# Final norm over all tiles with two experts still to come; the rows of the last two experts gathered, finished and written row by row into the output

## The chip, the cores and the metric

The kernel runs on one core of a Trainium2 chip. The time is device microseconds (us) of one execution. Five engines matter: TensorE (PE in the rows; its weight loads are PEld), VectorE (DVE), ScalarE (ACT), GpSimd (POOL) and SyncE (SP, which issues the plain DMAs). GpSimd also issues the indirect DMAs, which gather or scatter rows by a list of indices.

## What is computed

One layer of a decoder: a token mixer, then a mixture of 32 experts in which each token goes to two experts of one group, and a final RMS norm over the result. Only the end matters here:

```
out = jnp.zeros_like(tok)
for e in range(N_EXPERTS):
    hid = jax.nn.silu(tok @ w_gate[e]) * (tok @ w_up[e])
    out = out + combine[:, e:e + 1] * (hid @ w_down[e])
...
x = x + gate_f * out
return rmsnorm(x, norm_final)
```

with `rmsnorm(x, g) = x * rsqrt(mean(x * x) + EPS) * g`, over rows of 1024 values in f32. There are 1024 tokens, so the final norm has eight tiles of 128 rows.

## The kernel before

The kernel writes its instructions through a small scheduler of its own (`Sched`): each piece of work is a generator, which yields when it has to wait (for a time, or for a mark in `done`), and a modelled clock decides in which order the pieces put their instructions on the engines. On the chip each engine then runs its instructions in that order and waits on semaphores.

After the mixer and the router the residual rows stand in `x2d` in device memory and the normed rows in `h2d`. Each expert has a list of up to 96 tokens (`CAP`; `lists` holds tokens and weights, `LI["tok"]` the indices). For expert e the kernel gathers the listed rows of `h2d` (`gather`, an indirect DMA from GpSimd), transposes them on TensorE, multiplies by gate and up in three f32r passes, forms the product, multiplies by down (`down_gen`), and scales the result by the token's weight and gate row on VectorE (`y_gen`, `stt` into tile `y`). For experts 0 to 29 the 96 rows of `y` are then added to `x2d` by an indirect DMA that accumulates (`scatter`); each scatter waits until the one before has landed. The weights of all experts, 3 MB each, are loaded by SP and split in two on ScalarE and VectorE.

The last two experts, 30 and 31 (`NL = 2`), are not scattered. When the scatter of expert 29 is under way, `out_gen` starts: SP loads the eight tiles of `x2d` (into the weight buffers shown as HG, `fx` in the code) and the gain of the final norm (`nf`, shown as dn). The rows of experts 30 and 31 are put in place by TensorE instead: `sel_gen` has built, for each of the two, a 0/1 matrix that takes list places to tokens, and `y_mm` multiplies it with the two halves of `y` (tile `yw`, shown as ewx), eight matmuls for each of the eight output tiles. `out_fin` then handles a tile: add the loaded rows, square with a sum on ScalarE, the reciprocal root on GpSimd (`rstd_of`: a TENSOR_SCALAR and a TENSOR_TENSOR with pow, on 128x1), multiply by root and gain (one SCALAR_TENSOR_TENSOR on VectorE, for tiles 1 and 3 one on ScalarE and two on GpSimd), and store by SP into the output. No tile can be finished before expert 31 is multiplied by its down weights.

Of the kernel before, what the change touches and what calls it, by code (L numbers as in the profile page):

```python
# [19 lines left out]
P = 128  # L20
# [256 lines left out]
def build(tc, A, CB, CM, coff, out):  # L277
# [1452 lines left out]
    def gather(dst, idx):  # L1730
        LI["gat"] = G.indirect_dma_start(out=dst, out_offset=None, in_=h2d,
                             in_offset=bass.IndirectOffsetOnAxis(ap=idx, axis=0),
                             bounds_check=S - 1, oob_is_err=False)
        sch.note(G, 1.04)
        return sch.dma(dst.shape[0] * D * 4)
# [69 lines left out]
    def y_gen(e, py):  # L1805
# [13 lines left out]
        if e < NE - NL:  # L1819
# [9 lines left out]
            return  # L1829
        yw = yield from ews.take()  # L1830
# [7 lines left out]
        yts.put(y)  # L1838
        LI[("y", e)] = yw
        done.add(("y", e))  # L1840

    def sel_gen(mw):
        yield lambda: ("xT0", NE - NL + 1) in done
        for i in range(NL):
            sel = mw.tile([P, D], F32R, name="sel%d" % i, tag="xg%d" % i, bufs=1)
            tf, d8 = small([CAP, 1], "tf"), small([CAP, NT], "d8")
            ts(G, tf, lists[:, 0, EO[NE - NL + i]:EO[NE - NL + i] + 1], float(TOK0), OP.add)
            yield None
            ts(G, d8, iot[0:CAP, 0:NT], -float(P), OP.mult)
            ts(G, d8, d8, tf, OP.add)  # L1850
            yield None
            tt(V, sel[0:CAP].rearrange("p (t c) -> p t c", t=NT),
               iot[0:CAP, None, :].to_broadcast([CAP, NT, P]),
               d8[:, :, None].to_broadcast([CAP, NT, P]), OP.is_equal)
            LI["sel", i] = sel
            yield SEL_GAP
        done.add("sel")

    def out_gen():
# [12 lines left out]
        def slot(t):  # L1872
            if "pyL" in done and lvs.free():
                return lvs, 1
            if mms.free() > 1:
                return mms, 2
            if "hTL" in done and mss.free() > 1:
                return mss, 2

        for t in range(NT):  # L1880
            if t >= AHEAD:
                yield lambda: ("ym", t - AHEAD) in done
            yield lambda: slot(t) is not None
            res, n = slot(t)
            held = [res.tile() for _ in range(n)]
            p = held if n == 2 else [held[0][:, 0], held[0][:, 1]]
            if t in PREP:
                yield (f_at[t],)
                if "pyL" not in done:
                    yield lambda: "pyL" in done  # L1890
                for n in range(2):
                    mm(p[n], ident, fx[t][:, n * 512:(n + 1) * 512], True, False)
                yield (T_.free - LEAD,)
            for i in range(NL - 1):
                yield lambda: ("y", NE - NL + i) in done and "sel" in done
                y_mm(p, i, t, t not in PREP and i == 0)
                yield (T_.free - LEAD,)
            add(out_fin(t, res, held, p, fx[t], max(f_at[t], nf_at), nf))
            yield 0.0

    def y_mm(p, i, t, start):
        yw = LI[("y", NE - NL + i)]
        for h in range(2):
            for n in range(2):
                mm(p[n], LI["sel", i][0:CAP, t * P:(t + 1) * P], yw[0:CAP, h, n * 512:(n + 1) * 512],
                   start and h == 0, i == NL - 1 and h == 1)

    def out_fin(t, res, held, p, x, at, nf):
        yield lambda: ("y", NE - 1) in done and (t == 0 or ("ym", t - 1) in done)
        y_mm(p, NL - 1, t, False)  # L1910
        done.add(("ym", t), sch.t)
        yield (T_.free + LAT,)
        yield (at,)
        sq, rs = small([P, 2], "fsq"), small([P, 1], "frs")
        jk = nf[:, 1]
        if len(held) == 1:
            cols, p = [slice(0, D)], [held[0].rearrange("p b c -> p (b c)")]
        else:
            cols = [slice(0, 512), slice(512, D)]
        if t not in PREP:  # L1920
            for c, q in zip(cols, p):
                tt(V, x[:, c], q, x[:, c], OP.add)
            res.put(*held)
            yield None
            act(jk, x, AF.Square, accum_out=sq[:, 0:1])
            cols, p = [slice(0, D)], [x]
        else:
            for n, (c, q) in enumerate(zip(cols, p)):
                act(jk[:, c], q, AF.Square, accum_out=sq[:, n:n + 1])
            if len(p) > 1:  # L1930
                yield None
                tt(G, sq[:, 0:1], sq[:, 0:1], sq[:, 1:2], OP.add)
# [3 lines left out]
        if t >= NT - 1 and len(cols) == 1:  # L1936
            cols = [slice(0, 512), slice(512, D)]
            p = [p[0][:, c] for c in cols]
        for c, q in zip(cols, p):
            if t in POOL_T:  # L1940
                act(x[:, c], q, AF.Copy, scale=rs)
            else:
                stt(x[:, c], q, rs, nf[:, 0, c], OP.mult, OP.mult)
# [3 lines left out]
        if t in PREP:  # L1947
            res.put(*held)
# [335 lines left out]
```

## Time and profile before

| what | value |
|---|---|
| timed runs | 1141.23, 1144.24, 1150.05 us; median 1144.24 us |
| profiled execution | 1140.17 us, of which the span (first to last instruction) 1138.4 us |
| TensorE busy in the span | 1024.2 us (90%) |
| VectorE busy | 833.2 us (73%) |
| ScalarE busy | 521.3 us (46%) |
| GpSimd busy | 301.1 us (26%) |
| moved by DMA | 218.98 MB, mean 192 GB/s |
| mean granted TensorE clock | 0.966 |

Read it so: the profiler writes down one execution, with the start and the length of each instruction, and puts down each idle stretch of an engine to what ended it. Averages over the span say little about the last 40 us, where the change is made, so that stretch is read by itself. For an indirect DMA the length of the GpSimd instruction is not the transfer's; "to landing" is from its start until the data is there.

### The profile page before, as it was taken

Reading aid. Unit: us, or ns where it says so; the run is one execution under the profiler, and the core shown is the slowest. Engines: PE = TensorE matmul, PEld = TensorE weight load, DVE = VectorE, ACT = ScalarE, POOL = GpSimd, SP = SyncE. Lnnn points to the kernel's source line nnn. Section 1 sums busy time; section 2 is a strip of 40 time slices with the busy share of each in tenths; the row PEclk is TensorE's granted clock in tenths of the full one; section 3 lists DMA queues with packets and bytes.
Section 4 is the critical chain, followed back from the end, with each engine's and each line's share of the span. In section 5 each row is a group of like instructions: output and inputs, shape, how many; then the busy total and the mean of one; then the engine's idle time right before and its main releaser. Section 6 shows DMA issues by size and latency. Waiting matters only on the chain. (4 is left out here: it accounts for less than half of the span.)

```text
span 1138.4 us, 17044 instructions
## 1 busy us (share of the span) xinstructions
PE 1024.2 (90%) x6168; PEld 836.1 (73%) x6168; DVE 833.2 (73%) x1488; ACT 521.3 (46%) x981; POOL 301.1 (26%) x331
## 2 busy tenths in 40 slices
PE   3889999999989899998999998669999999999995
PEld 3779998899879888897898898546556555555554
DVE  6995776899997845459889887667666665757667
ACT  5423324556734323246555554355544444545434
POOL 4411220134411211102342212422332233433225
PEclk9899999999999999999999999879999999999998
DMA  9665557223214522134511189658999999999976
GB/s 310 188 190 186 163 165 237 56 56 94 80 42 132 169 83 56 43 100 131 172 56 57 55 295 337 237 153 254 298 293 322 305 318 308 316 319 317 312 227 260
DMA packets 96038, 218.98 MB, mean 192 GB/s; under 512 B 13342, under 2 KB 56538, under 8 KB 95954
## 3 DMA queue, kind: packets, MB, share of 16 engines
q1 hardware_dynamic: 89010, 201.67, 53.6%
q0 software_dynamic: 6944, 16.22, 6.3%
q8 instruction: 49, 0.80, 0.3%
q14 instruction: 35, 0.29, 0.1%
HBM read 201.64 MB, written 24.38 MB: 199 GB/s over the span
## 5 line engine op out<-in xcount | busy, mean ns | idle before, releaser
L220 PE MATMUL mm<-wg,HT 128*128 128x384 f32 (+2 forms) x1920 | 351.3, 335 | 19.3 <-DVE tmp L220 6.6
L220 PEld LDWEIGHTS mm<-wg,HT 128*128 128x128 f32 x1920 | 312.8, 193 | 31.1 <-issue 12.4
L220 PE MATMUL mm<-ew,xT 128*96 128x512 f32 x576 | 166.4, 427 | 7.8 <-DVE ew L220 6.1
L220 ACT ACTIVATE wg<-raw 128x768 fp32r<-128x768 f32 (+2 forms) x115 | 89.8, 782 | 144.3 <-PE mm L220 89.8
L220 DVE TENSOR_TENSOR wg<-raw,wg 128x768 fp32r<-128x768 f32 (+2 forms) x115 | 102.4, 890 | 62.2 <-ACT wg L220 61.8
L220 PEld LDWEIGHTS mm<-ew,xT 128*96 128x96 f32 x576 | 91.9, 165 | 61.6 <-issue 16.8
L220 DVE TENSOR_TENSOR ew<-HG,ew 128x1024 fp32r<-128x1024 f32 x68 | 81.3, 1218 | 34.3 <-ACT ew L220 34.3
L220 PE MATMUL lv<-rx 64*128 64x64 f32 (+5 forms) x1216 | 100.7, 278 | 5.5 <-DVE rx L220 3.7
L220 PEld LDWEIGHTS lv<-rx 64*128 64x128 f32 (+2 forms) x1216 | 89.1, 183 | 21.7 <-issue 15.0
L220 POOL DMA_INDIRECT x2d<-y,tki x30 | 64.7, 2158 | 144.6 <-DVE y L220 67.4
L220 PE MATMUL mm<-HT,wg 128*128 128x256 f32 (+1 forms) x576 | 97.2, 324 | 0.1
L220 ACT ACTIVATE ew<-HG 128x1024 fp32r<-128x1024 f32 x67 | 68.7, 1051 | 55.3 <-DMA HG<-expert_w_up 46.0
L220 PEld LDWEIGHTS mm<-HT,wg 128*128 128x128 f32 x576 | 82.1, 190 | 9.1 <-issue 1.0
L220 ACT ACTIVATE rx<-rx 128x64 f32<-128x64 f32 (+4 forms) x180 | 68.6, 418 | 31.8 <-DVE rx L220 19.6
L220 POOL DMA_INDIRECT xg<-h2d,tki x32 | 42.6, 1332 | 109.1 <-PE ms L220 98.2
L220 DVE SCALAR_TENSOR_TENSOR y<-lv,lists,GF 96x512 f32<-96x512 f32 x64 | 44.9, 740 | 31.2 <-PE lv L220 31.2
L220 PE MATMUL lv<-dn,hT 128*96 128x512 f32 x128 | 61.8, 606 | 2.0 <-ACT hT L220 2.0
L220 PE MATMUL lv<-dg,hT 128*96 128x512 f32 x128 | 60.1, 594 | 2.8 <-ACT hT L220 2.8
L220 PE MATMUL mm<-ewx,xT 128*96 128x512 f32 x192 | 59.9, 447 | 2.2 <-DVE ewx L220 2.0
L220 DVE TENSOR_TENSOR rx<-rx,qkc 128x320 f32<-128x320 f32 (+4 forms) x109 | 57.7, 563 | 0.8 <-ACT rx L220 0.8
L220 POOL TENSOR_TENSOR rx<-rx,qkc 128x256 f32<-128x256 f32 (+2 forms) x19 | 20.9, 1100 | 134.0 <-ACT rx L220 132.0
L220 PEld LDWEIGHTS ms<-cst,xg 96*128 96x128 f32 x256 | 34.5, 204 | 23.1 <-issue 13.3
(301 smaller groups left out, 1611.4 us busy)
## 6 DMA issues: line engine op xcount, KB each, us to landing
raw<-w_in SPq DMA_DIRECT2D x64, 384.0 KB, 3.3
HG<-expert_w_gate SPq DMA_DIRECT2D x46, 512.0 KB, 7.2
HG<-expert_w_up SPq DMA_DIRECT2D x46, 512.0 KB, 7.8
h<-w_ada SPq DMA_DIRECT2D x32, 512.0 KB, 4.4
dn<-expert_w_down SPq DMA_DIRECT2D x32, 512.0 KB, 8.4
dg<-expert_w_down SPq DMA_DIRECT2D x32, 512.0 KB, 8.8
raw<-w_out SPq DMA_DIRECT2D x26, 384.0 KB, 3.4
gu<-expert_w_gate SPq DMA_DIRECT2D x18, 512.0 KB, 6.4
```

The lines of the kernel that those rows point to most:

```text
L220: r = f(*a, **k)
```

## The change

- `sel_gen`, `y_mm` and their matrices are gone: six small GpSimd instructions, two 96x1024 ones on VectorE, and the 64 matmuls of 512 columns of `y_mm` with the two that brought tile 0 into the accumulator.
- `out_fin` no longer waits for experts 30 and 31. It norms each tile of `x2d` as it stands after expert 29 and stores it: eight full stores.
- `late_gen` and `late_rows` are new. When the scatter of expert 29 has landed, the rows of `x2d` that experts 31 and 30 will change are gathered into `xf` (two indirect DMAs). For expert 30 its `y` is added to its rows, normed, and written row by row into the output by an indirect DMA (`rows_out`). A token may stand in both lists; so a 96x96 matrix `both` (one small matmul and two small VectorE instructions; two 128x1024 fills on VectorE clear the tiles of the gathered rows beforehand) takes the rows of expert 30 to the places of expert 31, in four matmuls, and what comes out is added to the rows of expert 31, which are then normed and written the same way.
- `rows_out` waits until all eight stores have landed, and the second one also until the first row write has landed, since later writes replace earlier ones.

```
     def y_gen(e, py):
...
-        yw = yield from ews.take()
...
+        LI[("y", e)] = y
+        done.add(("y", e))
+    def rows_out(i, y, idx, nf):
+        yield lambda: all(("out", t) in done for t in range(NT))
+        for _ in range(i):
+            yield lambda: "rows0" in done
+        r = G.indirect_dma_start(out=outr, out_offset=bass.IndirectOffsetOnAxis(ap=idx, axis=0),
+                                 in_=y[0:CAP], in_offset=None, bounds_check=S - 1, oob_is_err=False)
+        after(r, LI["stores"] + ([LI["rows"]] if i else []))
...
+    def late_gen(mw, ml):
+        e0 = NE - NL
+        yield lambda: ("xT0", e0 - 1) in done
+        both = ml.tile([CAP, CAP], F32R, name="both")
+        xf = [mw.tile([P, D], F32, name="xf%d" % i, tag="xg%d" % i, bufs=1) for i in range(NL)]
+        V.memset(xf[0], 0.0)
+        V.memset(xf[1], 0.0)
...
+        ts(V, dg, ident[0:CAP, 0:CAP], lists[:, 0, e0 + 1:e0 + 2], OP.mult)
...
+        mm(pb[0:CAP, 0:CAP], ones[0:CAP, 0:CAP], dg, True, True)
...
+        tt(V, both, pb[0:CAP, 0:CAP], lists[:, 0, e0:e0 + 1].to_broadcast([CAP, CAP]), OP.is_equal)
...
+        yield lambda: ("scat", e0 - 1) in done
+        for i in (1, 0):
+            at = gather(xf[i][0:CAP], LI["tok"][:, e0 + i:e0 + i + 1], x2d)
...
+                mm(p[0:CAP, n], both, yw[0:CAP, h, n * 512:(n + 1) * 512], h == 0, h == 1)
...
+        add(late_rows(0, y, xf[0]), 0.0)
...
+            tt(V, xf[1][0:CAP, c], xf[1][0:CAP, c], p[0:CAP, n], OP.add)
...
+    def late_rows(i, y, xf):
...
+            tt(V, y[0:CAP, c], y[0:CAP, c], xf[0:CAP, c], OP.add)
...
+            act(xf[0:CAP, c], y[0:CAP, c], AF.Square, accum_out=sq[0:CAP, n:n + 1])
...
+        tt(G, sq[0:CAP, 0:1], sq[0:CAP, 0:1], sq[0:CAP, 1:2], OP.add)
+        ts(G, rs[0:CAP], sq[0:CAP, 0:1], 1.0 / D, OP.mult, EPS, OP.add)
+        tt(G, rs[0:CAP], rs[0:CAP], epsc[0:CAP, 0:1], OP.pow)
...
+        stt(y[0:CAP], y[0:CAP], rs[0:CAP], nf[0:CAP, 0], OP.mult, OP.mult)
...
+    def out_fin(t, x, at, nf):
+        sq, rs = small([P, 2], "fsq"), small([P, 1], "frs")
+        act(nf[:, 1], x, AF.Square, accum_out=sq[:, 0:1])
...
+        rstd_of(rs, sq[:, 0:1], D, 1)
...
+        stt(x, x, rs, nf[:, 0], OP.mult, OP.mult)
...
+        dma(outr[t * P:(t + 1) * P, :], x)
```

On VectorE the end of the program, from the scaling of expert 31's product on, reads before (lv and mm and ms are accumulators, HG the tiles of `x2d`, dn the gain, y the scaled product: the earlier number is expert 30, the later one expert 31):

```order
L220 SCALAR_TENSOR_TENSOR y_9937<-lv_9908,lists,GF 96x512 x2
L220 SCALAR_TENSOR_TENSOR y_9944<-lv_9932,lists,GF 96x512
L220 TENSOR_TENSOR ewx<-y_9937,ewx 96x512 x2
L220 SCALAR_TENSOR_TENSOR y_9944<-lv_9932,lists,GF 96x512
L220 TENSOR_TENSOR ewx<-y_9944,ewx 96x512 x2
L220 TENSOR_TENSOR HG_6699<-lv_9955,HG_6699 128x1024
L220 SCALAR_TENSOR_TENSOR HG_6699<-mm_9926,frs,dn_9899 128x512
L220 SCALAR_TENSOR_TENSOR HG_6699<-mm_9927,frs,dn_9899 128x512
L220 TENSOR_TENSOR HG_6699<-lv_9970,HG_6699 128x1024
L220 TENSOR_TENSOR HG_6699<-ms_9989,HG_6699 128x512
L220 TENSOR_TENSOR HG_6699<-ms_9990,HG_6699 128x512
L220 TENSOR_TENSOR HG_6303<-lv_10007,HG_6303 128x1024
```

and now, to the last wait of the tiles (y_9940 is expert 30, y_9950 expert 31, xf the gathered rows):

```order
L220 SCALAR_TENSOR_TENSOR y_9950<-lv_9932,lists,GF 96x512
L220 SCALAR_TENSOR_TENSOR HG_6699<-HG_6699,frs,dn_9886 128x1024 x2
L220 TENSOR_TENSOR ewx<-y_9940,ewx 96x512 x2
L220 SCALAR_TENSOR_TENSOR y_9950<-lv_9932,lists,GF 96x512
L220 SCALAR_TENSOR_TENSOR HG_6699<-HG_6699,frs,dn_9886 128x1024
L220 TENSOR_TENSOR y_9940<-y_9940,xf_9644 96x512 x2
L220 SCALAR_TENSOR_TENSOR HG_6699<-HG_6699,frs,dn_9886 128x1024
L220 SCALAR_TENSOR_TENSOR y_9940<-y_9940,frs,dn_9886 96x1024
L220 SCALAR_TENSOR_TENSOR HG_6303<-HG_6303,frs,dn_9886 128x1024 x4
L220 TENSOR_TENSOR xf_9645<-xf_9645,lv_9970 96x512 x2
L220 TENSOR_TENSOR y_9950<-y_9950,xf_9645 96x512 x2
L220 SCALAR_TENSOR_TENSOR y_9950<-y_9950,frs,dn_9886 96x1024
```

What moved: the eight full norm products now stand ahead of the last two additions to expert 31's rows, and expert 30's additions and product stand between those of tiles 2 and 4. Behind the last row shown there is only expert 31's own product (SCALAR_TENSOR_TENSOR, 96x1024).

On GpSimd the last rows before the closing barrier were these, with the semaphores that each waits for (the root of a tile is a TENSOR_SCALAR and a TENSOR_TENSOR):

```order
L220 TENSOR_TENSOR HG_6699<-HG_6699,dn_9899 128x512 [waits DMAHW1_49,DVE_49,Activation_49]
L220 TENSOR_SCALAR frs<-fsq 128x1 [waits Activation_49]
L220 TENSOR_TENSOR frs<-frs,epsc 128x1 [waits Pool_49]
L220 TENSOR_SCALAR frs<-fsq 128x1 [waits Activation_49]
L220 TENSOR_TENSOR frs<-frs,epsc 128x1 [waits Pool_49]
L220 TENSOR_TENSOR HG_6699<-HG_6699,dn_9899 128x512
L220 TENSOR_SCALAR frs<-fsq 128x1 [waits Activation_49]
L220 TENSOR_TENSOR frs<-frs,epsc 128x1 [waits Pool_49]
```

and are now these (DMAHW are the semaphores of SP's DMAs, DMASW those of GpSimd's):

```order
L220 TENSOR_SCALAR frs<-fsq 128x1 [waits DVE_49,Activation_49]
L220 TENSOR_TENSOR frs<-frs,epsc 128x1 [waits Pool_49]
L220 TENSOR_SCALAR frs<-fsq 128x1 [waits DVE_49,Activation_49]
L220 TENSOR_TENSOR frs<-frs,epsc 128x1 [waits Pool_49]
L220 TENSOR_SCALAR frs<-fsq 128x1 [waits DVE_49,Activation_49]
L220 TENSOR_TENSOR frs<-frs,epsc 128x1 [waits Pool_49]
L220 DMA out_dram<-y_9940,tki 1024x1024 [waits DMAHW4_49,DMAHW5_49,DMAHW3_49,DMAHW6_49,DMAHW2_49,DMAHW7_49,DMAHW1_49,DMAHW0_49]
L220 TENSOR_TENSOR fsq<-fsq 96x1 [waits Activation_49]
L220 TENSOR_SCALAR frs<-fsq 96x1 [waits DVE_49,Pool_49]
L220 TENSOR_TENSOR frs<-frs,epsc 96x1 [waits Pool_49]
L220 DMA out_dram<-y_9950,tki 1024x1024 [waits DMASW2_49,DVE_49]
```

What moved: GpSimd has no part of a tile's product any more. After the roots of the last tiles stands the row write of expert 30, which waits for SP's stores; the root of expert 31's rows stands behind it, and then the second row write, which waits for the first. The two gathers stand ahead of all the roots, right after the last scatter.

## Rows read from the trace of the kernel before

**Rows 1.** Busy time by stretch: start and end of the stretch, its length, then busy us (and instructions) of each engine, the granted clock, the share of the DMA engines and what they moved.

```profile
1070.00:1080.00 10.00, 8.53 (x42) 5.76 (x40) 7.22 (x10) 5.16 (x8) 4.83 (x7) 1.00 0.97 328
1080.00:1088.00 8.00, 7.61 (x23) 4.02 (x24) 7.22 (x9) 4.37 (x8) 0.00 (x0) 0.79 0.99 365
1088.00:1096.00 8.00, 8.00 (x29) 4.49 (x28) 6.58 (x8) 4.39 (x5) 4.48 (x1) 1.00 0.85 252
1096.00:1104.00 8.00, 8.00 (x32) 4.84 (x31) 2.34 (x4) 1.04 (x3) 1.42 (x1) 1.00 0.39 58
...
1132.00:1138.40 6.40, 0.00 (x0) 0.00 (x0) 1.42 (x2) 0.00 (x0) 0.38 (x1) 0.50 0.75 293
```

**Rows 2.** The chain of work that ended last, its pieces in order of time (start us, us, what), from the last down product on.

```profile
1102.95 5.15 PE lv L220 x12
1108.11 2.65 PE mm L220 x8
...
1112.70 0.94 PE lv L220 x4
...
1113.66 1.24 DVE HG L220
...
1128.76 1.86 POOL HG L220
1130.62 0.08 issue
1130.70 1.04 POOL frs L220
...
1132.41 0.75 DVE HG L220
```

**Rows 3.** The timeline of the end (start us, us, engine, line, operation, out<-in, count, idle before): the last scatter, the loads behind it, expert 30's and 31's products, the first and the last stores.

```profile
1098.49 1.42 POOL L220 DMA_INDIRECT x2d<-y,tki  x1 [4.63 <-DVE hid L220]
...
1104.09 0.80 SPq L295 DMA_DIRECT2D HG<-x2d  x2
1104.71 1.40 DVE L220 SCALAR_TENSOR_TENSOR y<-lv,lists,GF 96x512 f32<-96x512 f32 x2 [2.81 <-PE lv L220]
1104.95 0.42 SPq L295 DMA_DIRECT2D dn<-norm_final  x1
1105.41 3.17 SPq L295 DMA_DIRECT2D HG<-x2d  x6
...
1108.14 0.75 DVE L220 SCALAR_TENSOR_TENSOR y<-lv,lists,GF 96x512 f32<-96x512 f32 x1 [2.03 <-PE lv L220]
...
1130.64 4.13 SPq L295 DMA_DIRECT2D out_dram<-HG  x5
```

**Rows 4.** The output stores of SP as one group: length ns min/median/max, first and last start.

```profile
L295 SPq DMA_DIRECT2D out_dram<-HG x9: 332/338/923, 1116.4 to 1133.9; - x9
```

**Rows 5.** DMA, 1103 to 1119 us in 40 slices of 0.4 us (GB/s), then issues of the whole execution with size and median us from issue to landing, and the last scatter alone (1096 to 1106 us).

```profile
GB/s 72 0 0 0 0 215 164 379 389 451 348 420 328 225 205 266 246 369 420 440 399 430 410 430 410 420 440 400 440 410 420 410 420 400 420 410 410 410 420 318
...
out_dram<-HG SPq DMA_DIRECT2D x7, 512.0 KB, 3.4
h2d<-h SPq DMA_DIRECT2D x6, 512.0 KB, 2.8
xg<-h2d,tki POOLq DMA_INDIRECT x32, 8.7
x2d<-y,tki POOLq DMA_INDIRECT x30, 9.3
...
x2d<-y,tki POOLq DMA_INDIRECT x1, 5.5
```

**Rows 6.** Groups of instructions with one shape, after 700 us: count, busy us, mean ns of one, idle before.

```profile
L220 ACT ACTIVATE dn<-HG 128x1024 f32<-128x1024 f32 x7 | 7.4, 1054 | 2.9 <-DVE HG L220 2.7
L220 ACT ACTIVATION_READ_ACCUMULATOR dn<-HG 128x1 f32 x7 | 1.3, 186 | 0.0
L220 ACT ACTIVATE dn<-mm 128x512 f32<-128x512 f32 x2 | 1.2, 594 | 1.0 <-PE mm L220 1.0
L220 DVE SCALAR_TENSOR_TENSOR HG<-HG,frs,dn 128x512 f32<-128x512 f32 x2 | 1.4, 749 | 0.7 <-POOL frs L220 0.7
L220 DVE TENSOR_TENSOR HG<-lv,HG 128x1024 f32<-128x1024 f32 x5 | 6.1, 1215 | 2.1 <-PE lv L220 2.1
L220 DVE TENSOR_TENSOR HG<-ms,HG 128x512 f32<-128x512 f32 x2 | 1.3, 678 | 0.0
L220 DVE TENSOR_TENSOR ewx<-y,ewx 96x512 fp32r<-96x512 f32 x4 | 2.6, 681 | 0.1
L220 DVE SCALAR_TENSOR_TENSOR HG<-HG,frs,dn 128x1024 f32<-128x1024 f32 x4 | 7.8, 1974 | 0.1
L220 POOL DMA_INDIRECT xg<-h2d,tki x32 | 42.6, 1332 | 109.1 <-PE ms L220 98.2 <-issue 9.0 <-DVE cnt L220 1.7
```

**Rows 7.** The timeline of VectorE and GpSimd in two places where a full product and a root meet.

```profile
1120.49 1.29 POOL L220 TENSOR_TENSOR HG<-HG,dn 128x512 f32<-128x512 f32 x1
1120.56 2.31 DVE L220 SCALAR_TENSOR_TENSOR HG<-HG,frs,dn 128x1024 f32<-128x1024 f32 x1
...
1121.87 1.05 POOL L220 TENSOR_SCALAR frs<-fsq 128x1 f32<-128x1 f32 x1
...
1123.00 0.55 POOL L220 TENSOR_TENSOR frs<-frs,epsc 128x1 f32<-128x1 f32 x1
1123.64 0.19 POOL L220 TENSOR_SCALAR frs<-fsq 128x1 f32<-128x1 f32 x1
...
1131.83 0.55 POOL L220 TENSOR_TENSOR frs<-frs,epsc 128x1 f32<-128x1 f32 x1
1132.41 1.42 DVE L220 SCALAR_TENSOR_TENSOR HG<-HG,frs,dn 128x512 f32<-128x512 f32 x2 [0.71 <-POOL frs L220]
```

**Rows 8.** The place of the new fills and of `both`: GpSimd's own fill of a tile of that shape, and VectorE at expert 28 (1058 to 1066 us); then the idle stretch of TensorE that follows (1077 to 1082 us).

```profile
L220 POOL MEMSET xg<- 128x1024 f32 x2 | 1.8, 952 | 0.1
...
1062.07 0.41 DVE L220 TENSOR_TENSOR hid<-hid,mm 96x256 f32<-96x256 f32 x1
1063.33 2.35 DVE L220 TENSOR_TENSOR ewx<-HG,ewx 128x1024 fp32r<-128x1024 f32 x2
...
1080.39 0.90 PE L220 MATMUL ms<-cst,xg 96*128 96x96 f32 x4 [1.85 <-ACT hT L220]
```

More of the change, by code (lines that the diff above doesn't have):

```diff
@@ L1728, in build, with gather @@
     NXG = 4
[L1730 to L1731 removed]
+    def gather(dst, idx, src=None):
+        LI["gat"] = G.indirect_dma_start(out=dst, out_offset=None, in_=h2d if src is None else src,
                              in_offset=bass.IndirectOffsetOnAxis(ap=idx, axis=0),
@@ L1829, in y_gen, with after @@
             return
+        LI[("y", e)] = y
+        done.add(("y", e))
+    def after(r, firsts):
+        for first in firsts:
+            tc.add_manual_dep(r.ins, first.name,
+                              mybir.DependencyInfo(mybir.DependencyClass.Sync, mybir.DependencyReason.DATA),
+                              reason="rows written again")
+    def rows_out(i, y, idx, nf):
[5 more added lines that the diff above has]
+        after(r, LI["stores"] + ([LI["rows"]] if i else []))
+        LI["rows"] = r.ins
+        done.add("rows%d" % i)
+    def late_gen(mw, ml):
[5 more added lines that the diff above has]
+        V.memset(xf[1], 0.0)
+        hid = yield from hds.take()
+        dg = hid[0:CAP, 0:CAP]
+        ts(V, dg, ident[0:CAP, 0:CAP], lists[:, 0, e0 + 1:e0 + 2], OP.mult)
+        yield None
+        pb = yield from mss.take()
+        mm(pb[0:CAP, 0:CAP], ones[0:CAP, 0:CAP], dg, True, True)
+        hds.put(hid)
+        yield None
+        tt(V, both, pb[0:CAP, 0:CAP], lists[:, 0, e0:e0 + 1].to_broadcast([CAP, CAP]), OP.is_equal)
+        mss.put(pb)
+        yield lambda: ("scat", e0 - 1) in done
+        at = 0.0
+        for i in (1, 0):
+            at = gather(xf[i][0:CAP], LI["tok"][:, e0 + i:e0 + i + 1], x2d)
+        yield lambda: ("y", e0) in done and "nf" in LI
+        y = LI["y", e0]
         yw = yield from ews.take()
@@ L1837, in y_gen @@
             tt(V, yw[0:CAP, 1, c], y[0:CAP, c], yw[0:CAP, 0, c].bitcast(F32), OP.subtract)
[L1838 to L1857, printed above, removed]
+        yield None
@@ new lines, in late_gen @@
+        yield lambda: lvs.free() > 0
+        p = lvs.tile()
+        for n in range(2):
+            for h in range(2):
+                mm(p[0:CAP, n], both, yw[0:CAP, h, n * 512:(n + 1) * 512], h == 0, h == 1)
+        ews.put(yw)
+        add(late_rows(0, y, xf[0]), 0.0)
+        yield (max(at, T_.free + LAT),)
+        for n in range(2):
+            c = slice(n * 512, (n + 1) * 512)
+            tt(V, xf[1][0:CAP, c], xf[1][0:CAP, c], p[0:CAP, n], OP.add)
+        lvs.put(p)
+        yield None
@@ L1870, in out_gen @@
                     nf_at = dma(nf[:, 0], A["norm_final"].rearrange("(o n) -> o n", o=1).to_broadcast([P, D]))
[L1872 to L1878, printed above, removed]
-        for t in range(NT):
[L1881 to L1913, printed above, removed]
-        sq, rs = small([P, 2], "fsq"), small([P, 1], "frs")
[L1915 to L1932, printed above, removed]
@@ L1933, in out_fin @@
+        LI["nf"], LI["stores"] = nf, []
+        for t in range(NT):
+            yield (f_at[t],)
+            add(out_fin(t, fx[t], max(f_at[t], nf_at), nf))
+            yield 0.3
+    def out_fin(t, x, at, nf):
+        sq, rs = small([P, 2], "fsq"), small([P, 1], "frs")
+        act(nf[:, 1], x, AF.Square, accum_out=sq[:, 0:1])
         yield None
@@ L1935, in out_fin @@
         yield None
[L1936 to L1943, printed above, removed]
-            if t >= NT - 1:
-                yield None
-                dma(outr[t * P:(t + 1) * P, c], x[:, c])
-        if t in PREP:
-            res.put(*held)
-        yield None
-        if t in POOL_T:
-            for n in range(2):
-                c = slice(n * 512, (n + 1) * 512)
-                tt(G, x[:, c], x[:, c], nf[:, 0, c], OP.mult)
-                yield None
-        if t < NT - 1:
-            dma(outr[t * P:(t + 1) * P, :], x)
+        yield (at,)
+        stt(x, x, rs, nf[:, 0], OP.mult, OP.mult)
+        yield None
+        dma(outr[t * P:(t + 1) * P, :], x)
+        LI["stores"].append(sch.ld)
         done.add(("out", t))
@@ L2109, in main_gen @@
         drop(pool_l, wp, omp)
-        mw = rpool("mw")
+        mw = LI["mw"] = rpool("mw")
         ews.extend(mw, "ew", E_GRAN)
@@ L2123, in main_gen @@
         add(x_gen(gxs))
-        add(sel_gen(mw))
         yield 0.15
@@ L2143, in main_gen @@
         yield 0.1
+        add(late_gen(LI["mw"], ml))
         add(down_gen())
```

13 lines of the change are left out of this document (added).

## Prediction

> **What bounds the kernel now.** I read the busy time by stretch first, to see which stretch the change can touch. Until 1080 us the DMA engines are at 0.97 and TensorE has gaps; from 1088 on the weights are in, TensorE is busy 8.00 of 8 us twice in a row, and in the last 6.4 us only stores move [rows 1]. So the end is bound by what follows the last products, not by weights. The chain of waits tells what that is: the last down products end at 1108, then come the matmuls that put the rows of experts 30 and 31 into the tiles, and from 1113.66 on a relay of VectorE, ScalarE and GpSimd over eight tiles, to the last product at 1132.41 [rows 2]. The last store starts at 1133.9 [rows 4] and lands 3.4 later [rows 5], at 1137.3; the span closes 1.1 behind it, at 1138.4. Thirdly the timeline: the last scatter starts at 1098.49 [rows 3] and lands 5.5 later [rows 5]; at 1104.09 SP begins to load the eight tiles [rows 3]. That moment is where the new path starts, since the tiles no longer wait for experts 30 and 31.
>
> **What is removed.** The relay of [rows 2], and with it the 66 placing matmuls, the eight additions into the tiles and the two tiles that GpSimd multiplied. In the middle two 96x1024 VectorE instructions and six small ones on GpSimd go. I give nothing for these: TensorE, which would have to become faster by it, runs without a gap from 1088 to the last down product [rows 1, 2], and neither takes work from it.
>
> **What is added before the end.** Two fills, two small VectorE instructions and a small matmul at expert 28. VectorE has no fill of that shape; it costs between nothing and what GpSimd takes, 0.95 each, 1.9 together [rows 8]. I take nothing: the weights still come in then, and TensorE waits 1.85 at 1080 anyway [rows 8]. Without that cover it would be up to 1.9 on the end.
>
> **The new path, step by step.** The last scatter is unchanged, so loads and gathers start at 1104.1.
>
> Loads: in the row of slices the first two tiles (1.05 MB) are in by 1108, the gain (the slow slices of 205 to 266 GB/s) by about 1109.8, and all 4.7 MB by 1117.8 [rows 5]. The gathers share the engines. By the problem's sizes a list holds 64 tokens on average, 0.26 MB, 0.64 us each at the 410 GB/s of the later slices (an estimate). So the gain lands near 1110.8 and the last tile near 1119.
>
> First product: the square of tile 0 (1.05 and 0.19 for the sum [rows 6]) from 1107.8, its root (0.19 and 0.55 [rows 7], some 0.16 between) to 1110. The gain is later, and the root of tile 1 gets in the way: the first product starts at about 1111.2.
>
> Length of a product: 0.749 for 512 columns; from 512 to 1024 columns an addition grows from 0.678 to 1.215, by 0.54 [rows 6]; so 1.29. The 1.97 that the group shows for 1024 columns [rows 6] holds waits for GpSimd, next paragraph but one.
>
> VectorE from 1111.2 in its new order: tiles 0 and 1 (2.58), expert 30's two subtractions (1.36), half of expert 31's scaling (0.75), tile 2 (1.29), expert 30's two additions (1.36), tile 3 (1.29): 8.6, and 0.6 for roots in between: 1120.5. Expert 30's squares (0.59 and 0.19, twice [rows 6]) end inside tile 3's product, its root takes three GpSimd instructions, to 1121.5; its product ends at 1122.8. Since it stands in order, tiles 4 to 7 wait behind it, though their squares are done.
>
> Tiles 4 to 7: here the place that decides. A root that came up while VectorE multiplied two tiles of SBUF took 1.05 in place of 0.19 and ended 0.05 behind that product; and a product that started inside GpSimd's work took 2.31 [rows 7]. GpSimd runs the root of the next tile only between two products, and VectorE starts 0.03 after a root (1131.83 + 0.55, then 1132.41), GpSimd's next root 0.09 after (1123.00 + 0.55, then 1123.64) [rows 7], so VectorE is first. They alternate: 1.29, then 0.05 + 0.08 + 0.55 + 0.03 = 0.7 for the root (0.08 between its two instructions), 2.0 a tile. Tile 4 runs 1123.5 to 1124.8, tile 7 ends at 1130.8. If they overlapped freely it would be 1122.8 + 4 x 1.29 = 1127.9.
>
> The Trainium skill has this as a rule: in "SBUF — State Buffer", section "Who interferes with whom", a VectorE instruction with two SBUF inputs and a GpSimd instruction that reads SBUF exclude each other, and the one that comes second waits for the whole of the first. The trace agrees (1.05 against 0.19). By that rule the end is 1143.9, without it 1141.0.
>
> Last store: 3.4 to landing [rows 5], 1134.2. The copies themselves don't bind: loads and gathers to 1119, 4.19 MB of stores at 410 GB/s to 1129.3, 1129.9 with the landing.
>
> Row writes: GpSimd waits for all stores, so the first starts at 1134.3. No plain indirect write stands in the trace. Below it costs 2.8, a plain store of 512 KB [rows 5]; above 5.5, the accumulating scatter of the same rows with the queue empty [rows 5]. I take 4.2: GpSimd's 1.42 for the issue [rows 3] and 2.8 for a plain store. It lands at 1138.5. The second waits for it and lands at 1142.8; with 1.1 to close: 1143.9. Expert 31's own chain hides under the first write, just: four additions (2.7) to 1133.5, squares to 1134.3, GpSimd free at 1135.7, root to 1136.9, product to 1138.2. If it came later, each microsecond would count.
>
> The sum: 1143.9 against 1138.4, +5.5 us. The freed relay is worth much less than it looks, because the new end has the stores of all tiles and two full landings one behind the other. The profiled execution took 1140.17, 1.8 more than its span: 1145.7. It lies 4.1 below the median of 1144.24; on the median the sum is 1149.7.
>
> **Rivals.** A, the above: 1143.9. B, roots and products don't exclude each other in the small: 1141.0, 1146.8 on the median. For it: many roots took 0.19 [rows 7]; against it, none of those met a product. C, the copies bind: stores land at 1129.9, two row writes of 2.8, end at 1136.6, 1.8 less than before (1142.4 on the median). It needs both lower bounds and VectorE ahead of the stores. D, a row write costs what a scatter took on the median in this kernel, 9.3 [rows 5]: two of them add 10.2, 1154.1, 15.7 slower (1159.9 on the median). Its place is the two landings; from 7.2 each on it decides (4.2 and half of 11.4 - 5.5). For it: the median; against it: those ran among weight loads, and the one in the empty queue took 5.5.
>
> That the change gains over 1% (11.4 us) would need an end before 1127.0; the stores alone land at 1129.9. Only a change in the stages before could do that.
>
> **How the numbers follow.** A 0.50, B 0.25, C 0.05, D 0.14, something before the end that shifts the time by over 1% either way 0.03 each. Within 1% (about what a measurement of this kernel can tell from no change): A, B, C, 0.80; slower 0.17; faster 0.03. The range reaches from below C, 1141, to row writes of 7.8 each, 1157; A's own, with row writes of 2.8 to 5.5, is 1147 to 1152.
>
> **What would show it.** Products of tiles 4 to 7 that start 2.0 apart, not 1.3. Roots of about 1 us among them. The first row write at about 1134, behind the last store's landing, and the second some 4 later, with the end 5 behind that. TensorE's last matmul (with `both`) before 1118. I am wrong where tile 7's product ends before 1128, where the two row writes start less than 3 or over 7 apart, or where the loads of the tiles don't start at 1104.

## The result, and the profile after

| | before | after |
|---|---|---|
| median of 22 runs each | 1141.28 us (1134.87 to 1152.42) | 1148.00 us (1141.30 to 1157.24) |
| profiled execution, its span | 1140.17, 1138.4 us | 1147.61, 1145.5 us |

The ratio of after to before is 1.0065, with a 95% interval of 1.0040 to 1.0091: 7.4 us slower (4.6 to 10.4). 5.5 had been forecast. That is under the 1% (11.4 us), and on the side that was forecast.

First what the change did where it touches the stretches of [rows 1]. The windows of the changed kernel (same columns as there):

```profile
1088.00:1096.00 8.00, 8.00 (x31) 4.76 (x30) 6.29 (x7) 3.72 (x5) 0.94 (x1) 1.00 0.73 218
1096.00:1104.00 8.00, 8.00 (x29) 4.25 (x28) 1.62 (x4) 1.04 (x3) 2.38 (x2) 1.00 0.37 59
1104.00:1112.00 8.00, 2.73 (x7) 0.76 (x5) 1.95 (x3) 3.34 (x6) 2.53 (x6) 0.87 0.92 314
...
1132.00:1140.00 8.00, 0.00 (x0) 0.00 (x0) 1.75 (x2) 1.29 (x4) 2.97 (x5) 0.50 0.17 52
1140.00:1145.50 5.50, 0.00 (x0) 0.00 (x0) 0.00 (x0) 0.00 (x0) 0.00 (x0) 0.50 0.15 43
```

TensorE is still full until 1104 and then done: the placing matmuls are gone. But the last 13.5 us are nearly empty on every engine, and the DMA engines stand at 0.17 and 0.15. The kernel waits there; it does not work. The timeline shows for what. It answers to [rows 3] and [rows 7] (start us, us, engine, line, operation, out<-in, count, idle before and what ended it):

```profile
1102.29 0.80 SPq L295 DMA_DIRECT2D HG<-x2d  x2
...
1111.07 2.48 DVE L220 SCALAR_TENSOR_TENSOR HG<-HG,frs,dn 128x1024 f32<-128x1024 f32 x2 [4.03 <-DMA dn<-norm_final]
...
1124.80 1.28 DVE L220 SCALAR_TENSOR_TENSOR HG<-HG,frs,dn 128x1024 f32<-128x1024 f32 x1 [0.72 <-POOL frs L220]
1124.84 1.28 POOL L220 TENSOR_SCALAR frs<-fsq 128x1 f32<-128x1 f32 x1
...
1126.21 0.55 POOL L220 TENSOR_TENSOR frs<-frs,epsc 128x1 f32<-128x1 f32 x1
1126.79 1.28 DVE L220 SCALAR_TENSOR_TENSOR HG<-HG,frs,dn 128x1024 f32<-128x1024 f32 x1 [0.71 <-POOL frs L220]
...
1128.79 1.28 DVE L220 SCALAR_TENSOR_TENSOR HG<-HG,frs,dn 128x1024 f32<-128x1024 f32 x1 [0.71 <-POOL frs L220]
...
1133.67 1.01 POOL L220 DMA_INDIRECT out_dram<-y,tki  x1 [4.92 <-DMA out_dram<-HG]
...
1138.21 0.99 POOL L220 DMA_INDIRECT out_dram<-y,tki  x1 [2.37 <-DMA out_dram<-y,tki]
```

To be read: the products of the last tiles start 2.0 apart, and each time GpSimd's small step (a 128x1 instruction, 0.19 by itself in [rows 7]) takes 1.28 beside the product. The last tile product ends at 1130.07. The first row write starts 3.6 behind it, when the last store has landed; the second starts 4.54 behind the first; then come 7.3 more to the end. The pieces of the chain of waits that ended last, answering to [rows 2], are now landings:

```profile
1130.11 2.60 DMA out_dram<-HG
...
1133.67 3.72 DMA out_dram<-y,tki
...
1137.97 1.23 POOLq L2269
```

Since both profiles start the tile loads at different times (1104.09 and 1102.29), I measure from there what the change touches: the **tail**, from the first load of the residual stream to the end of the span. Before it is 1138.4 - 1104.09 = 34.3, after it is 43.2. To the end of VectorE's last tile product it is 29.7 before (1132.41 + 1.42) and 27.8 after, so the relay did become 1.9 shorter; from there to the end it is 4.6 before and 15.4 after. 10.8 - 1.9 = 8.9 us. What lies ahead of the tail took the same in these two profiles: from the first gather of the expert stage (737.07 and 735.05) to the first load 367.0 and 367.2.

### The profile page after: what moved, and what is told of

It reads as the page before. It is cut to its first block, busy times and chain, and to the rows that moved or that the text cites. A ratio compares the mean times of both kernels' runs of the same rounds, so it can differ in the third digit from the quotient of the medians.

```text
span 1145.5 us, 16937 instructions
## 1 busy us (share of the span) xinstructions
PE 1009.5 (88%) x6106; PEld 823.9 (72%) x6106; DVE 829.5 (72%) x1487; ACT 521.1 (45%) x983; POOL 294.0 (26%) x330
## 5 line engine op out<-in xcount | busy, mean ns | idle before, releaser
L220 DVE TENSOR_TENSOR ew<-HG,ew 128x1024 fp32r<-128x1024 f32 x68 | 81.3, 1218 | 31.6 <-ACT ew L220 31.4
L220 POOL DMA_INDIRECT x2d<-y,tki x30 | 61.3, 2043 | 149.8 <-DVE y L220 82.1
L220 DVE SCALAR_TENSOR_TENSOR y<-lv,lists,GF 96x512 f32<-96x512 f32 x64 | 45.0, 741 | 33.4 <-PE lv L220 33.3
L220 POOL DMA_INDIRECT xg<-h2d,tki x32 | 40.0, 1250 | 113.3 <-PE ms L220 102.7
L220 PEld LDWEIGHTS ms<-cst,xg 96*128 96x128 f32 x256 | 34.4, 203 | 20.9 <-issue 13.3
```

Source lines behind the costliest of these rows:

```text
L220: r = f(*a, **k)
```

## The experiments

Tails come from one profile each, ratios from the timed runs against the kernel before on the same chip.

| run | tail, us | ratio to before, 95% interval |
|---|---|---|
| before / after | 34.3 / 43.2 | 1.0065 [1.0040, 1.0091] |
| e1 no row writes | 38.5 | 1.0016 [0.9988, 1.0044] |
| e2 one row write | 39.7 | 1.0033 [1.0000, 1.0066] |
| e3 no gathers | 42.2 | 1.0040 [1.0010, 1.0069] |
| e4 gain in PSUM | 41.5 | 1.0047 [1.0020, 1.0074] |
| e5 no writes, no last root | 34.7 | 0.9987 [0.9956, 1.0018] |
| e6 gain loaded first | 42.2 | 1.0036 [1.0012, 1.0061] |
| e7 rows ready before the writes | 41.9 | 1.0071 [1.0039, 1.0103] |
| e8 two writes at once | 38.5 | 1.0005 [0.9980, 1.0031] |
| e11 as e8, early gathers | 40.2 | 1.0017 [0.9991, 1.0043] |
| e9 before, gain in PSUM | 35.7 | 1.0021 [0.9986, 1.0056] |
| e10 as e9, copies later | 30.8 | 0.9931 [0.9906, 0.9955] |
| e12 as e10, gain loaded first | 31.9 | 0.9988 [0.9965, 1.0011] |

**e1 and e2: the row writes.** The call that writes the rows is taken out, in e1 for both experts and in e2 for expert 31.

```diff
-        r = G.indirect_dma_start(out=outr, out_offset=bass.IndirectOffsetOnAxis(ap=idx, axis=0),
-                                 in_=y[0:CAP], in_offset=None, bounds_check=S - 1, oob_is_err=False)
-        after(r, LI["stores"] + ([LI["rows"]] if i else []))
...
```

> Leaves out both row writes; experts 30 and 31 are computed and normed, and their rows not written, so the end is the landing of the last tile store. Theory (two row writes one behind the other, and a slow close behind the last of them, stand at the end of the chain): the first row write started at 1133.67 in the changed kernel, right behind the last store's landing, and the close behind a store took 1.1 in the kernel before, so a span near 1134.8, 10.7 us less than the changed kernel's 1145.5, and a ratio to the kernel before of about 0.997. Rival (the row writes cost only what a plain store costs, 2.8 each, and the rest of the loss is the gathers and the alternation): 5.6 less, 1139.9, ratio about 1.0015.

> Leaves out the second row write alone (expert 31's rows are computed and not written). Theory (behind an indirect DMA GpSimd needs some 5.5 us from the end of its issue before it can close, whether the data has landed or not, so the close costs 3.6 instead of 1.1): the time falls by the distance of the two writes alone, 4.5 us, span near 1141.0, ratio about 1.0025; GpSimd's closing drain ends about 5.5 after the issue. Rival (the second write landed late, or the close was slow by chance): the span ends 1.1 behind the first write's landing at 1137.4 to 1138.0, so 1138.5 to 1139.1, 6.4 to 7.0 less, ratio about 1.0005.

Measured: both theories missed. e1 took 4.7 off the tail, where the theory had 10.7 and the rival 5.6; e2 took 3.5 off, where the theory had 4.5 and the rival 6.4 to 7.0. In e1 the last store starts at 1126.7 and has landed by 1131, and yet the span ends at 1137.2. What stands there is GpSimd's closing DRAIN, one of the instructions that end the program on each engine (its shortest, middle and longest length in ns, then first and last start). Before, after and e1, the last with the root that stands ahead of it:

```profile
L2279 POOLq DRAIN  x3: 40/114/5748, 1131.8 to 1138.1; - x3
L2279 SPq DRAIN  x3: 7/7/7, 1137.3 to 1137.8; - x3
```

```profile
L2269 POOLq DRAIN  x3: 40/114/6692, 1138.0 to 1145.2; - x3
L2269 SPq DRAIN  x3: 7/7/7, 1142.2 to 1144.9; - x3
```

```profile
1130.46 0.54 POOL L220 TENSOR_TENSOR frs<-frs,epsc 96x1 f32<-96x1 f32 x1
...
L2265 POOLq DRAIN  x3: 40/114/5908, 1130.4 to 1136.9; - x3
```

The long one is queued behind GpSimd's last instruction and ends 5.2 to 5.5 after that instruction's end: before, the last root ends at 1132.38 and the DRAIN at 1131.8 + 5.75 = 1137.5; after, the second write's issue ends at 1139.20 and the DRAIN at 1144.7; in e1, the last root ends at 1131.00 and the DRAIN at 1136.3. (Two kernels with two writes in flight at the end, e8 and e11 below, have 5.8 to 5.9.) The span ends 0.8 to 0.9 later. So the close is 6.0 to 6.3 behind GpSimd's last instruction, whether that is a DMA (after) or a small root (before, e1, e2). In the kernel before it doesn't show, because SP's wait for the last store ends at 1137.3, 0.2 ahead of the DRAIN. After, SP is through with its own wait at 1142.2, and the DRAIN goes on for 2.5.

**e5: the test of that.** Without row writes, and expert 31's three small GpSimd instructions out too, so that GpSimd ends with tile 7's root.

```diff
-        tt(G, sq[0:CAP, 0:1], sq[0:CAP, 0:1], sq[0:CAP, 1:2], OP.add)
...
+        if i:
+            rs = sq
...
```

> Leaves out both row writes, as the run without them did, and expert 31's three small GpSimd instructions as well (its product is then taken with a number that is not the root; it still stands on VectorE). GpSimd's last instruction is now tile 7's root, some 4.5 us earlier than expert 31's. Measured from the start of the first load of the residual stream to the end of the span (the run without row writes: 38.5 us). Theory, that the program ends some 6.2 us after GpSimd's last instruction of any kind: the tail falls by 4 to 6 us, to 32.5 to 34.5, where the landing of the last store (28.05 + 3.4 to 4.2 + 1.1) binds as well; GpSimd's closing DRAIN ends 5.2 to 5.5 us after tile 7's root. Rival, that the run without row writes ended on VectorE's last product or on something that the three instructions have no part in: the tail stays at 38 to 39.

Measured: tail 34.7, 3.8 below e1, for three instructions of 0.9 us together. VectorE's last product ends 33.7 after the first load in both runs, so it wasn't what ended e1. The theory stands, the rival (38 to 39) falls. It came 0.2 above the range I gave, because the next thing now binds: VectorE's last product ends at 1136.01 + 1.28 = 1137.3, behind the DRAIN's 1130.9 + 5.91 = 1136.8.

```profile
1130.89 0.55 POOL L220 TENSOR_TENSOR frs<-frs,epsc 128x1 f32<-128x1 f32 x1
...
L2268 POOLq DRAIN  x3: 40/114/5913, 1130.9 to 1138.1; - x3
L2268 SPq DRAIN  x3: 7/7/7, 1137.4 to 1137.7; - x3
...
L2268 DVEq DRAIN  x2: 19/670/1320, 1136.0 to 1137.8; - x2
```

**e3 and e6: what makes the first product late.** It came 8.8 after the first load, 7.1 were forecast. In e3 the gathers are out, in e6 the gain's load stands ahead of the tile loads.

```diff
-            at = gather(xf[i][0:CAP], LI["tok"][:, e0 + i:e0 + i + 1], x2d)
+            at = 0.0
```

> Leaves out the two gathers of rows; experts 30 and 31 are added to zeros, so their rows come out without the residual. Theory (the gathers hold up the loads of the tiles by more than their bytes: the slices fell from 410 to about 290 GB/s while they ran): gain and tile 2 land 1.7 and 3.8 us earlier after the start of the loads, the first product starts about 7.1 after the first load instead of 8.8, tile 3's product ends 2 earlier and so does the end: span about 1143.5, ratio about 1.0048. Rival (the gathers cost their 0.58 MB only, 1.4 us, and VectorE's order hides that): 0 to 0.5 less, and tile 2 lands at most 1.4 earlier.

```diff
+        nf_at = dma(nf[:, 0], A["norm_final"].rearrange("(o n) -> o n", o=1).to_broadcast([P, D]))
         fx, f_at = {}, {}
...
```

> One edit: the gain's load is issued ahead of the eight tile loads and not after the first two. All work is kept. In the profile of the change the first two products stood ready for the gain for 4.0 us and came 8.8 after the first load's start, 1.7 later than forecast. Theory, that this lateness hardly reaches the end, since tile 2's square came after it anyway (its load landed 11.75 after the start) and the products from there go at the pace of the exclusion (2.0 each): first product 6.5 to 7.5 after the first load's start, tail from the first load 42.7 to 43.3 against 43.2. Rival, that the gain's landing sets VectorE's whole row of products: the tail falls by 1.5 or more, to 41.7 or less.

Measured: in e3 the first product comes 8.82 after the first load, no earlier, and the tail is 1.0 shorter, between the theory's 2 and the rival's 0.5 at most. Yet e3 does not clear the gathers, for its transfers stop while the gain is under way. The GB/s of the changed kernel and of e3, in slices of 0.4 us from the first load:

```profile
GB/s 0 0 195 82 420 379 440 440 389 287 256 215 195 246 256 369 399 287 287 287 287 318 287 277 287 256 307 256 307 317 410 399 420 410 410 410 410 410 410 410
```

```profile
GB/s 0 0 133 143 348 389 430 430 379 410 174 10 10 0 0 92 328 338 369 420 338 461 389 440 420 410 430 399 461 379 451 410 420 420 399 420 399 420 399 430
```

From 4.4 to 6.0 us behind the first load e3 moves 10 GB/s or less; only e11 has such a gap too, and what makes it no run tells. In the kernels without gathers among the loads and without the gap (e7, e8, e9) the copies that wait for the gain start 6.8, 7.4 and 7.2 after the first load; with the gathers there (after, e1, e2, e4, e5) the gain is used from 8.7 to 9.6 on. These profiles suggest that the gathers hold the gain back by some 2 us, where 1.3 of bytes had been reckoned, and e3's 1.0 is not their price.

With the gain's load first (SP issued it at 1088.19, 15 us ahead of the tiles) the first product comes at 5.5, and the tail is 42.2, 1.0 shorter: below the range of the theory and above the rival's. So 1.0 of the 3.3 us reaches the end. But e6 does not move the gain alone. Tile 2's square and product in the change, then the first product and tile 2's square in e6:

```profile
1114.04 1.06 ACT L220 ACTIVATE dn<-HG 128x1024 f32<-128x1024 f32 x1 [4.93 <-DMA HG<-x2d]
...
1116.13 1.29 DVE L220 SCALAR_TENSOR_TENSOR HG<-HG,frs,dn 128x1024 f32<-128x1024 f32 x1 [0.71 <-POOL frs L220]
```

```profile
1108.75 1.28 DVE L220 SCALAR_TENSOR_TENSOR HG<-HG,frs,dn 128x1024 f32<-128x1024 f32 x1 [0.38 <-POOL frs L220]
...
1112.21 1.06 ACT L220 ACTIVATE dn<-HG 128x1024 f32<-128x1024 f32 x1 [2.36 <-DMA HG<-x2d]
```

In the change tile 2's square waits for its load until 11.75 after the first load, and VectorE then 0.71 for tile 2's root. In e6, with the gain's 0.5 MB out of the way, that square starts at 9.0. The 1.0 is what the gain among the loads costs, by its own lateness and tile 2's together; the run does not separate them.

**e4: roots and products.** The gain is copied into PSUM, so each product reads only one operand from SBUF.

```diff
...
+        gp = yield from lvs.take()
+        LI["gp"] = gp = gp.rearrange("p b c -> p (b c)")
+        yield (nf_at,)
+        for n in range(2):
+            act(gp[:, n * 512:(n + 1) * 512], nf[:, 0, n * 512:(n + 1) * 512])
...
-        stt(x, x, rs, nf[:, 0], OP.mult, OP.mult)
+        stt(x, LI["gp"], rs, x, OP.mult, OP.mult)
```

> The final gain is copied once into PSUM by ScalarE, and each product reads the gain from there, so VectorE reads one operand from SBUF instead of two; the product of expert 30's rows with the matrix goes to two other accumulators. The result is the same. The order at the start of the tiles shifts a little with it. Theory (VectorE's product with two SBUF operands and GpSimd's root exclude each other): the roots of tiles 4 to 7 take 0.2 us instead of 1.28, the products start 1.3 apart instead of 2.0, and tile 7's product ends about 3 earlier; span about 1142.5, ratio about 1.004. Rival (the distance of 2.0 is the latency of the relay square, root, product, not an exclusion): roots and distances stay, no change.

Measured, in the timeline of e4:

```profile
1120.54 6.04 DVE L220 SCALAR_TENSOR_TENSOR HG<-lv,frs,HG 128x1024 f32<-128x1024 f32 x5
...
1121.97 0.19 POOL L220 TENSOR_SCALAR frs<-fsq 128x1 f32<-128x1 f32 x1 [0.37 <-DVE HG L220]
1122.24 0.55 POOL L220 TENSOR_TENSOR frs<-frs,epsc 128x1 f32<-128x1 f32 x1
```

Five products are 1.21 apart, and the roots take 0.19 in the middle of them. The exclusion is shown, and the rival falls. The tail got only 1.7 shorter, for three reasons: the products start late, 14.7 after the first load, since ScalarE's copies wait for the gain ahead of the squares; they bunch at the end, so that their stores take 4.2 from the last start (1126.6) to the first row write (1130.75); and everything behind is as it was.

**e7, e8, e11: can the end be shortened?** e7 takes e4, puts both experts' rows behind the eight tile products and ahead of both writes, and the gathers behind tile 1's product. e8 also takes the shared tokens out of expert 30's list, so that the second write needn't wait for the first. e11 is e8 with the gathers back at the loads. Parts of e8's edit:

```diff
+        V.tensor_reduce(fl, both.bitcast(F32), AX, OP.add)
...
+        stt(fl, fl, 2048.0, lists[:, 0, e0:e0 + 1], OP.mult, OP.add)
...
+        ts(V, ix, fl, float(TOK0), OP.add)
...
+        for k in range(2):
+            r = G.indirect_dma_start(out=views[k], out_offset=bass.IndirectOffsetOnAxis(ap=LI["ix"][k], axis=0),
...
+            after(r, LI["stores"])
```

> The gain in PSUM (1.21 a product instead of 2.0 with its wait), the two gathers issued after the loads and first products, expert 30's and 31's additions, squares, roots and products all behind the eight tile products, and then the two row writes, the second still waiting for the first one's landing. All work is kept. Tail from the first load's start, 43.2 with the change and 41.5 with the gain in PSUM alone: tile 7's store starts at 22 to 24, the experts' rows are ready some 5.5 later, at about 28, the stores have landed by then (4.2); writes at 28 and 32.5, the last issue ends at 33.5 and GpSimd's close takes 6.2: 39.7 (38 to 41), a ratio to before of 1.004. Rival, that the 8 stores' transfers bind (bunched stores took 4.2 to land, and would take longer still): first write at 30 or later, tail 41.5 or more, no better than the gain alone.

> As the kernel with the gain in PSUM and both experts' rows ready first, but the tokens that both experts have are taken out of expert 30's list (three small VectorE instructions in the MoE stage), so the two row writes go to different rows and neither waits for the other. All work is kept. Theory: a second write costs its issue (1.0 to 1.1) and not the 4.5 of the first one's landing; writes at about 28 and 29.1 after the first load's start, last issue ends at 30.1, close 6.2: tail 36.3 (34.5 to 38), about 3.4 less than with the second write waiting; ratio to before 1.000 to 1.003. Rival, that two writes in flight hold each other up or that the close waits for landings that then come later: tail 38 or more.

> The kernel with two row writes at once, with the gathers back where the change has them, at the first loads. All work is kept. With the gathers behind tile 1's product GpSimd's two issues (2.4 us) stood ahead of tile 5's root, and VectorE's products paused 2.4. Theory: that pause goes and the loads land up to 1.4 later instead, the experts' rows are ready some 1 earlier; tail 37.5 (36.5 to 38.2) against 38.5; ratio to before 0.999 to 1.003. Rival, that the loads' bytes bind: tail 38.5 or more.

Measured. e7 missed (41.9): tile 7's store did start at 22.2 after the first load, but the first row write only at 30.2, as VectorE waited for the gathers until 1127.27, 8.8 behind the first one's issue. That is the rival's number (41.5 or more), but the write itself waited for VectorE and not for the stores, whose last bytes moved by 1130.6. e8's tail is 38.5, above its range and inside the rival's (38 or more). It is 3.5 below e7 (38.48 against 41.94), where the second wait was reckoned at 3.4; its two writes stand back to back:

```profile
1137.09 1.02 POOL L220 DMA_INDIRECT out_dram<-y,ix  x1 [0.60 <-DVE y L220]
1138.41 0.93 POOL L220 DMA_INDIRECT out_dram<-y,tki  x1 [0.30 <-issue]
```

So the writes do not hold up each other's issue. What takes e8 out of its range is the first write, at 29.5 and not 28, and the close, 6.8 behind the second's issue and not 6.2. e11 came out at 40.2, in the rival's range. The products run without a pause, but the gain lands 11.1 after the first load and not 7.4 (ScalarE's copies start at 1115.79 and at 1115.00), and the first product starts at 14.4 and not 10.7. Since e11's transfers have the gap of e3, it is not shown that the gathers' bytes alone do this. The best of these, e8, comes out level with the kernel before by the time, 1.0005, though its tail is 4.2 longer (more on that in the next section).

**e9, e10, e12: the kernel before with the gain in PSUM.** [rows 7] show the same exclusion in the kernel before. e9 has e4's copies there; in e10 they come behind the split of expert 31's product; e12 has e6's early gain too. Parts of e10's edit (in e9 the first line of `to_psum` waits for `"pyL" in done` instead):

```diff
+        def to_psum():
+            yield lambda: ("y", NE - 1) in done and lvs.free() > 0
+            gp = lvs.tile()
...
+            for n in range(2):
+                act(gp[:, n * 512:(n + 1) * 512], nf[:, 0, n * 512:(n + 1) * 512])
...
-                stt(x[:, c], q, rs, nf[:, 0, c], OP.mult, OP.mult)
...
+                    stt(x[:, c], LI["gp"][:, c], rs, x[:, c], OP.mult, OP.mult)
```

> The kernel before, with one thing of the experiments: the gain is copied into PSUM by ScalarE once expert 31's product has left its banks, and the VectorE products of tiles 2 and 4 to 7 read it there. All work is kept. In the kernel before, three of these products take 2.04 to 2.31 instead of 1.2 and GpSimd's small steps 1.05 instead of 0.19. Theory, that VectorE's products with two SBUF operands and GpSimd shut each other out: products 1.2, no root step of 1.05 beside them, tile 7's last store 1 to 2 earlier measured from the first load of the residual stream (28.3 before or so), tail 32.5 to 33.3 against 34.3; ratio 0.998 to 1.000. Rival, that the banks given up (one pair less for the tiles' matmuls) or ScalarE's two copies of 0.6 bind instead: tail 34.3 or more.

> The kernel before with the gain in PSUM, as tried, with one thing mended: ScalarE's two copies come behind the split of expert 31's product and no longer ahead of it, where they held it for the gain's landing (5.12 of waiting; the split came 8.4 after the first load's start where the kernel before has it at 6.7). All work is kept. Tails so far: before 34.3, with the copies ahead 35.7. Theory: TensorE's row of selections starts 1.7 to 2.0 earlier and the exclusion is gone from the products, tail 33.3 to 34.2, a ratio to before of 0.999 to 1.000, too little to tell by the time. Rival, that the pair of banks given up for the gain holds TensorE's selections back: tail 34.5 or more.

> The kernel before with the gain in PSUM behind expert 31's split, and the gain's load ahead of the tile loads. All work is kept. The run with the gain in PSUM alone had a tail of 30.9 against 34.3, -3.4 us, which would be a ratio of 0.997, but its time came out at 0.9931 [0.9906, 0.9955], more than the tail explains. Theory, that only the tail is changed by these edits and that the rest of that number is the scatter of the expert stage from execution to execution: tail 30.0 to 31.0 (the gain's 0.5 MB leave the loads' queue; ScalarE did not wait for it), ratio 0.995 to 0.999. Rival, that the gain in PSUM brings something ahead of the tail too: ratio 0.993 or less again, with the first load of the residual stream 3 us or more earlier than the 1104.1 of the kernel before.

Measured. In e9 the tail got longer, 35.7, as the rival had it, though no first step of a root takes over 0.20 any more. What ate the saving is neither the banks nor the 0.6 of a copy: the copies waited 5.12 for the gain, and expert 31's split stood behind them in ScalarE's queue.

```profile
1115.48 1.23 ACT L220 ACTIVATE lv<-dn 128x512 f32<-128x512 f32 x2 [5.12 <-DMA dn<-norm_final]
...
1116.64 1.14 ACT L220 ACTIVATE ewx<-y 96x512 fp32r<-96x512 f32 x2
```

In e10 that is mended. Its timeline, at the place of [rows 7], where the product took 2.31:

```profile
1120.37 1.30 POOL L220 TENSOR_TENSOR HG<-HG,dn 128x512 f32<-128x512 f32 x1
1120.44 1.28 DVE L220 SCALAR_TENSOR_TENSOR HG<-lv,frs,HG 128x1024 f32<-128x1024 f32 x1 [0.23 <-POOL frs L220]
```

The same two instructions meet in the same way, and neither waits. The tail is 30.8, 3.5 below before and better than I expected (33.3 to 34.2). By the time e10 gained 7.9 (5.1 to 10.7), more than the tail has, and e12 1.4 (4.0 gained to 1.3 lost) with a tail of 31.9. Measured from expert 30's scaling (1104.71, 1104.57 and 1106.11), which TensorE sets and not the loads, the end comes 33.7 later before, 30.5 in e10 and 30.5 in e12. So 3.2 us are shown in the traces, and the early gain adds nothing to it. e12's first load lies at 1104.75, so nothing ahead of the tail moved: the rival falls, though its tail is 0.9 above my range, since its loads came 1.4 ahead of TensorE and not 0.3. That the two timings differ by more than their intervals stays open. e10 has the lowest ratio of this study; what it has beyond the 3.2 us is not explained.

## Why the prediction was right, and where it was off

All times here are from the first load of the residual stream; the forecast had it at 1104.1.

| step | forecast | measured |
|---|---|---|
| first product | 7.1 | 8.8 |
| tile 7's product ends | 26.7 | 27.8 |
| first row write | 30.2 | 31.4 |
| second row write | 34.4 | 35.9 |
| end | 39.8 | 43.2 |

- **The loads, the gain.** Loads at 1102.29 and not 1104.1: this execution was 2.0 earlier at the first gather of the expert stage already. The first product was 1.7 late. My reading of the slices took the gain's bytes as all in by 1109.8, 5.7 after the first load, and added 1.0 for the gathers. Without gathers among the loads the gain came at 6.8 to 7.4 (e7, e8, e9), with them at 8.7 to 9.6: the reading was 1.1 to 1.7 short, and the gathers seem to take more than their bytes. Nor had I reckoned with a wait for tile 2's load, 11.75 behind the first. At tile 7 this left 1.1 of the 3.4 that are missing.
- **The order and the length of a product.** 1.28 for the forecast 1.29, in the group of the page that answers to [rows 6]:

```profile
L220 DVE SCALAR_TENSOR_TENSOR HG<-HG,frs,dn 128x1024 f32<-128x1024 f32 x8 | 10.2, 1283 | 7.6 <-DMA dn<-norm_final 4.0 <-POOL frs L220 3.6
```

- **The place that decides, tiles 4 to 7.** 2.0 a tile, as forecast, and not 1.29: rival B falls, and e4 and e10 show the cause by taking it away. The rule cited in the prediction (the Trainium skill, "SBUF — State Buffer", "Who interferes with whom") says also that a VectorE instruction with at most one SBUF input, outside what it calls the 2-port perf modes, doesn't contend with GpSimd; the trace agrees, 1.28 beside 1.30 in e10 against 2.31 in [rows 7].
- **Stores and row writes.** From the last store's start (1130.1) to the first write 3.6, forecast 3.4 and 0.1; the chain puts 2.6 of it to the landing. Write to write 4.54, forecast 4.2, made of other parts: 1.01 for the issue and not 1.42, 3.72 from the start to the landing, 0.8 from there to the second's start. Rivals C (2.8) and D (9.3) fall.
- **The term that was mis-sized: "1.1 to close".** From the second write's landing to the end I took the 1.1 of the kernel before. By that the end would have come at 35.9 + 3.7 + 1.1 = 40.7; it came at 43.2. The close hangs on GpSimd's last instruction, 6.3 behind it here. This is 2.5 of the 3.4 (1.1 stand in tile 7, 0.1 and 0.3 in the two writes, and the second landing gave back 0.5). It also means that the landing of the second write bound nothing: its issue did.
- **The middle, put at nothing.** VectorE took 0.91 for each fill at expert 28, and in the two profiles the expert stage was not longer (367.2 against 367.0).

```profile
L220 DVE MEMSET xf<- 128x1024 f32 x2 | 1.8, 912 | 0.3 <-issue 0.3
```

All profiles together leave room for a saving there. From the first gather to the first load they have 360.2 to 367.2 in the ten kernels built on the change (mean 364.8) and 366.7 to 368.3 in the four built on the kernel before (mean 367.2). And in nine of the ten the time shows 1.5 to 4.0 us less loss than the tail (e3: 4.6 against 7.9; e8: 0.6 against 4.2). So the change may save some 2 us ahead of the tail; with one profile of each kernel this is not shown.

The time came within 1.7 of the forecast (1148.0 against 1149.7) partly because the median of three runs that it started from was 3.0 above that of 22. The difference of the two kernels was 5.5 forecast, 7.4 by the times and 8.9 by the tails of the two profiles. So the mechanism was right; the close was sized too small, and the loads were read as in too early.

## What to carry to other kernels

Count the landings that stand one behind the other at the end of a kernel: taking work out of a relay bought 1.9 here, and two writes that had to wait for it, and for each other, cost 10.8 with the close. Ask of every engine when its last instruction ends, GpSimd's above all: here everything it does late is paid for with 6 us more, and leaving three small instructions out at its end was worth as much as a row write (3.8 against 3.5). Where VectorE multiplies two SBUF tiles beside small GpSimd steps, one operand in PSUM took the wait away in both kernels, but what is queued behind the copy that puts it there has to be looked at (e9 against e10).

## What the runs showed of the hardware that was not expected

- GpSimd's closing DRAIN ends 5.2 to 5.5 us behind its last instruction, in every kernel here where one write or none was in flight at the end, and 5.8 to 5.9 where two were (e8: 1138.0 + 7.22 against 1139.34; e11: 1136.3 + 7.75 against 1138.21). VectorE's ends with its last instruction (after: 1135.9 + 1.32, the product 1135.88 + 1.28), and SP's take 7 ns. Why GpSimd's takes that long no run here tells.
- The same instructions ahead of the tail take a different time from execution to execution: the first tile load started between 1098.65 (e1) and 1108.94 (e3), in kernels that differ only behind it. That is as much as the whole effect, and the reason for measuring from the load.
- In two of the fourteen profiles (e3, e11) the transfers behind the first tile loads stop for 1.6 us, at 20 GB/s or less from 4.4 to 6.0 us behind the first load. Both have a late gain. The cause is open.
